# Another order of products in one stage of a TensorE-bound block, a root spread by two float32r products, and a bias moved to the output gate

## The chip, the cores and the metric

The kernel runs on one core of a Trainium2 chip. The metric is the device time of one execution, in microseconds (us). The profile of one execution gives, for each engine, when each instruction ran: TensorE (PE, with its weight loads PEld), VectorE (DVE), ScalarE (ACT), GpSimd (POOL) and the DMA-issuing SyncE (SP).

## What is computed

One block over 512 tokens of width 1024, in float32. The change lies in the middle part, the token mixer:

```python
h = RMSNorm(x); p = h @ w_in             # one input projection
r, k, v, w_lo, a_lo, g_lo = token_shift(p[:, :SHIFT_COLS], mu)   # u + (prev - u) * mu, columns of 512, 512, 512, 64-wide codes, ...
w_log = -softplus(-(w0 + tanh(w_lo) @ w_up)) - 0.5               # decay
a     = sigmoid(a0 + a_lo @ a_up)                                # rate
g     = sigmoid(g_lo) @ g_up
... delta-rule recurrence over 8 heads of 64, giving y ...
y = groupnorm(y) * lnx_g + lnx_b
y = (y + sum(r * k * r_k) * v) * g                               # bonus, output gate
```

A second mixer (forgetting attention), two SwiGLU layers and a final norm make up the rest.

## The kernel before

Everything is kept transposed: 128 features on the partitions, 512 tokens in the free dimension (P = 128, T = 512, KD = 8 slices of the model width, NB = 4 blocks of 128 tokens, NP = 4 pairs of heads). A float32 product is made of three float32r products: each operand is split into a rounded high part and the rest, and `mm3` (L174 to L176) adds hi*hi, lo*hi and hi*lo in one PSUM bank. The weights' split is `split_w`: ScalarE casts `raw` to `whi` (L166), VectorE subtracts to `wlo` (L167). `raw` has three buffers, filled by SP's queue; `whi` and `wlo` have two each. A projection column of 128 outputs is `mix.cols`: 8 slices of 3 products, 24 in all, into one bank named `pk` (mixer columns), `pl` (codes), `pgt` (gates) or `pq`.

The stage with the change begins near 340 us with the codes (`psa`, `psg`). VectorE and ScalarE make the mixer norm's reciprocal root for each token (`root`); TensorE spreads it over all partitions by a product with a matrix of ones (`spread_root`, tile `rows`), and VectorE copies it to `rstd`. Every later column is multiplied by `rstd` when it leaves its bank (tile `u`), then token-shifted by a ScalarE scale and a VectorE multiply-add (`shifted`). The codes go through tanh and a cast to the tile `codes`. Meanwhile TensorE makes the first pair's k column (weights at DA) and r column (at 0); their results go to `spare1`. Then four pairs of products with 96-row operands, the tiles `pz`, give decay and rate for the four pairs of heads (`uw`, `ux` are the up-projections, prepared by GpSimd; `za` holds the results), each followed by a sigmoid on ScalarE.

Four steps follow, `step(p)`, one for each pair of heads. Each has its columns k, r and v and one gate column `pgt`, the normalization of the keys (`ksq`, its parts `khi` and `klo`, the sum `pn`, and `krn`), the decayed products, the products `gp` of keys with queries (64 records of 64x64), and the bonus: `rk`, its parts `rhi` and `rlo`, the sum over a head by two products into `pn`, and `bon`, stored to `bsave` and read back at the end, where `shaped` and `opened` apply it and the gate. The third column of the first pair, v, takes the weights loaded in advance as `ready[2 * DA]`.

In this stage the order of each engine's instructions isn't written by hand: the tile framework's scheduler orders them from its own estimate of times, except where `tc.issue_after` (this instruction after that one on its engine) or `tc.keep_in_program_order` binds it. Every engine runs its instructions in that order. From about 500 us on the order is written out by hand.

Of the kernel before, what the change touches and what calls it, by code (L numbers as in the profile page):

```python
# [10 lines left out]
F32R = mybir.dt.float32r  # L11
BF16 = mybir.dt.bfloat16
AF = mybir.ActivationFunctionType
ALU = mybir.AluOpType
# [4 lines left out]
P = 128  # L19
T = 512  # L20
D = 1024
KD = D // P
DFF = 2816
KF = DFF // P
DA = 512
NP = DA // P
C = 32
NC = T // C
NB = T // P
# [4 lines left out]
PAR_FFN1, PAR_MIX, PAR_FFN2, PAR_MU = 0, 8, 16, 24  # L34
PAR_MUA, PAR_MUG = 36, 37
PAR_W0, PAR_A0, PAR_KK, PAR_KA, PAR_RK, PAR_LG, PAR_LB = 38, 42, 46, 50, 54, 58, 62
# [45 lines left out]
def kernel(  # L82
# [24 lines left out]
    dve, act, pe = [Queued(e, False) for e in (nc.vector, nc.scalar, nc.tensor)]  # L107
# [10 lines left out]
    pr = ctx.enter_context(tc.tile_pool(name="pr", bufs=3, space=PSUM))  # L118
    pf = ctx.enter_context(tc.tile_pool(name="pf", bufs=3, space=PSUM))
    dp = ctx.enter_context(tc.tile_pool(name="dp", bufs=1, space=DRAM))  # L120

    def bank(name, pool_=None):
        pool_ = pool_ or pm
        return pool_.tile([P, T], F32, tag="b", name=name)

    def tmp(name, shape=(P, T), dt=F32, tag="t", **kw):
        return tp.tile(list(shape), dt, tag=tag, name=name, **kw)


    ident = cp.tile([P, P], F32, name="ident")  # L130
# [3 lines left out]
    onesr = cp.tile([P, P], F32R, name="onesr")  # L134
    ones = onesr[:].bitcast(F32)
# [34 lines left out]
    def load_w(aps, kt, n, eng=None):  # L170
        return split_w(load_raw(aps, kt, n), kt, n, eng)
# [23 lines left out]
    def split(dst_hi, dst_lo, src, hi_eng="act"):  # L195
        cast = act.copy(dst_hi, src) if hi_eng == "act" else dve.tensor_copy(dst_hi, src)
        return cast, dve.tensor_tensor(dst_lo, src, dst_hi.bitcast(F32), op=ALU.subtract)

    def f32(ap):
        return ap.bitcast(F32)  # L200
# [7 lines left out]
    class Plan:  # L208
# [4 lines left out]
        def op(s, engine, us, do, *deps, rank=0, takes=(), frees=(), later=0.0, kind="w"):  # L213
            s.ops.append(dict(engine=engine, do=do, deps=deps, takes=takes, frees=frees, done=False))
            return s.ops[-1]
# [86 lines left out]
    def pc(i):  # L302
        return par[:, i:i + 1]
# [345 lines left out]
    class Wide:  # L649
# [231 lines left out]
        def root(s):  # L881
            nrm = s.nrm
            for i in range(2):
                pe.matmul(s.ssum[:], onesr[:], nrm.sum[i][:], start=i == 0, stop=i == 1)
            nrm.rstd = xp.tile([P, T], F32, tag="rstd", name="rstd")
            act.activation(nrm.rstd[:], s.ssum[:], AF.Ln, bias=epsr[:, 0:1], scale=1.0 / D)
            act.activation(nrm.rstd[:], nrm.rstd[:], AF.Exp, scale=-0.5)
            s.sa = [xp.tile([P, T], F32, tag="acc", name=f"sa{i}", bufs=2)[:] for i in range(2)]
# [83 lines left out]
    mix = Norm(PAR_MIX, 2)  # L972
# [45 lines left out]
    def root(rc):  # L1018
        dve.tensor_tensor(rc, sums[0][:], sums[1][:], op=ALU.add)
        act.activation(rc, rc, AF.Ln, bias=epsr[:, 0:1], scale=1.0 / D)  # L1020
        act.activation(rc, rc, AF.Exp, scale=-0.5)
        dg = tmp("dg")
        for b in range(NB):
            dve.tensor_scalar(dg[:, b * P:(b + 1) * P], ident[:], rc[:, b:b + 1], None, op0=ALU.mult)
        return dg

    def spread_root(dg, behind):
        ps = bank("rows", pr)
        with tc.issue_after(behind.ins):
            pe.matmul(ps[:], ones, dg[:], start=True, stop=True)  # L1030
        mix.rstd = xp.tile([P, T], F32, tag="rstd", name="rstd")
        dve.tensor_copy(mix.rstd[:], ps[:])

# [7 lines left out]
    op = o1.enter_context(tc.tile_pool(name="o1", bufs=1, side="right"))  # L1041
# [33 lines left out]
    def win(c0, n=P):  # L1075
        return [(0, W[:, c0:c0 + n])]

    nrm2 = Norm(PAR_FFN2)
    with ExitStack() as mx:
        rp = mx.enter_context(tc.tile_pool(name="rp", bufs=1))  # L1080
# [5 lines left out]
        def duo(tag, name, dt=F32):  # L1086
            return sp.tile([P, 2, T], dt, name=name, tag=tag)
# [3 lines left out]
        spare = [h[:, i] for h in (duo("RD2", "spare0"), duo("RD3", "spare1")) for i in range(2)]  # L1091
# [10 lines left out]
        def shifted(o, src, rows, mu):  # L1102
            act.activation(o[0:rows, :], src[0:rows, :], AF.Copy, scale=omu[0:rows, mu - PAR_MU:mu - PAR_MU + 1])
            dve.scalar_tensor_tensor(o[0:rows, 1:T], src[0:rows, 0:T - 1], pc(mu)[0:rows, :], o[0:rows, 1:T],
                                     op0=ALU.mult, op1=ALU.add)


        rc = rp.tile([P, NB], F32, name="rc")
# [28 lines left out]
        uw, ux = [lr.tile([96, DA], F32R, name=n) for n in ("uw", "ux")]  # L1137
# [13 lines left out]
        def normed(ps, rows=P):  # L1151
            u = tmp("u")
            dve.tensor_tensor(u[0:rows, :], ps[0:rows, :], mix.rstd[0:rows, :], op=ALU.mult)
            return u
# [13 lines left out]
        ready = {c0: load_w(win(c0), KD, P) for c0 in (DA, 0)}  # L1168
        act.on, act.last = True, None
        ready[2 * DA] = load_w(win(2 * DA), KD, P)  # L1170
        lw, lx = [codes[:, i] for i in range(2)]
# [6 lines left out]
        act.on = False  # L1178
        zslots = [h for g in G[3] for h in (g[:, 0:8], g[:, 8:16])] + [BKs[3][:, 0:8], BKs[3][:, 8:16]]
        zslots = [h.rearrange("p c a t -> p (c a t)") for h in zslots] + spare[0:2]  # L1180
        spread = []
        for o, c0, mu in ((spare[2], DA, 4), (spare[3], 0, 0)):
            ps = bank("pk", pf)
            spread = mix.cols(ps[:], *ready.pop(c0), P)
            shifted(o, normed(ps), P, PAR_MU + mu)
        za = []
        for p in range(NP):
            za.append((zslots[2 * p], zslots[2 * p + 1]))
            for i, (w_, x_, par0, o) in enumerate(((uw, lw, PAR_W0, zslots[2 * p]), (ux, lx, PAR_A0, zslots[2 * p + 1]))):
                ps = bank("pz", (pr, pf)[i])  # L1190
                with tc.issue_after(spread[2 * p + i].ins):
                    pe.matmul(ps[:], w_[0:96, p * P:(p + 1) * P], x_[0:96, :], start=True, stop=True)
                tc.keep_in_program_order(act.activation(o, ps[:], AF.Sigmoid, bias=pc(par0 + p)))
        logs = tc.keep_in_program_order(act.preload_act_table_set("natural_log_exp_and_others"))
        xctx.close()
        fctx = ExitStack()
        vtp = fctx.enter_context(tc.tile_pool(name="vtp", bufs=1, side="right"))
# [10 lines left out]
        vs = [V4[:, p] for p in range(NP)]  # L1208
# [10 lines left out]
        def work(name, dt=F32):  # L1219
            late = name in ("kka", "rk", "bon")  # L1220
            return t2.tile([P, T], dt, name=name, tag="sb" if late else "sa", bufs=3 if late else 5)
# [48 lines left out]
        def half(q):  # L1270
            return slice(q * 64, (q + 1) * 64)

        def step(p):
            if p % 3 == 0:
                k, r = spare[2], spare[3]
            else:
                k, r = [t2.tile([P, T], F32, name=f"{n}{p}")[:] for n in "kr"]
# [26 lines left out]
            ps = bank("pn", pf)  # L1304
# [20 lines left out]
            with tc.issue_after(mms[5].ins):  # L1325
                for c in range(NC):
                    for q in range(2):
                        o = half((q + c + 1) % 2)
                        gm = pe.matmul(gps[q][o, c // 2], BK[half(q), c], G[p][0][half(q), c], start=True, stop=True)
            for q in range(2):  # L1330
                for odd in range(2):
                    o = half((q + odd + 1) % 2)
# [4 lines left out]
                        op=ALU.mult)  # L1337
# [9 lines left out]
            ps = bank("pn", pr)  # L1347
# [4 lines left out]
                pe.matmul(ps[:], bonesr[:], lo[:], start=False, stop=True)  # L1352
            bon = work("bon")
            dve.tensor_tensor(bon[:], ps[:], v[:], op=ALU.mult)
            act.activation(bon[:], bon[:], AF.Identity, bias=pc(PAR_LB + p))
            nc.sync.dma_start(bsave[p], bon[:])

        for p in range(NP):
# [13 lines left out]
        for t in range(C - 1):  # L1372
            n, m = t + 1, C - 1 - t
# [82 lines left out]
        for b in range(NB):  # L1456
            o = vtp.tile([P, T], F32, name=f"vt{b}", tag=f"vt{b}")
# [39 lines left out]
        for q in range(2):  # L1497
            o = (1 - q) * 64
# [11 lines left out]
        for q in range(2):  # L1510
            o = (1 - q) * 64
# [9 lines left out]
        for q in range(2):  # L1521
            pool.memset(Rs[0][half(q), :, q, :], 0.0)
            for i in range(RN):
                o = (1 - q) * 64
# [6 lines left out]
        op = plan.op  # L1531
        summed, gone = [op("SP", 0.0, None, later=us, frees=frees) for us, frees in ((3.0, ()), (3.5, ["w"]))]
        o = op("ACT", 0.69, b1.log, summed, rank=SCAN, takes=["t"], frees=["pf"])
        o = op("ACT", 0.63, b1.root, o, rank=SCAN)
# [110 lines left out]
        for c in range(NC):  # L1645
# [4 lines left out]
            if c % 4 == 3 and c < NC // 2:  # L1650
                o = op("SP", 0.4, on(fetch, nc.sync, c + 5, 4), e, later=4.0)
# [15 lines left out]
        ready, weighed = {0: [summed], 1: [rooted]}, []  # L1667
# [72 lines left out]
        for m in range(NP + 3, 2 * KD):  # L1740
            g = Held()
            w, o = columns("pgt", COL_GA + m * P)
# [11 lines left out]
            o = op("DVE", 0.61, result, o, rank=NEXT, takes=["gs"], frees=["pm"])  # L1754
            if m + 1 < 2 * KD:
                o = op("ACT", 0.55 if tanhs else 1.84, opened, o, *roots, rank=ROWS)
# [150 lines left out]
        o = []  # L1907
        for p in range(NP):
            o = op("ACT", 0.63, on(part_y, p), *outs[p], *sees, *o, rank=FILL)
            o = [op("DVE", 0.69, on(part_l, p), o, rank=FILL)]  # L1910
# [29 lines left out]
        ycs, sqs, pgs, pus, parts = [None] * NP, [None] * NP, [None] * NP, [None] * NP, {}  # L1940
# [30 lines left out]
            dve.scalar_tensor_tensor(vs[p], vs[p], pc(PAR_LG + p), bons[p], op0=ALU.mult, op1=ALU.add)  # L1971

        def opened(p):
            dve.tensor_tensor(vs[p], vs[p], pus[p][:], op=ALU.mult)

        def halves_of(p):
            split(*ya[p], vs[p])
# [33 lines left out]
        ps = proj(0, fox_proj, ybs, fws[0])  # L2011
        for m in range(KD):
# [11 lines left out]
            if m + 1 < KD:  # L2024
                ps = proj(m + 1, fox_proj, ybs, fws[m + 1])
# [29 lines left out]
        for m in range(KD):  # L2055
            g = slot[m]
            ps = proj(m, rwkv_proj, ya)
# [4 lines left out]
        for m in range(KD):  # L2062
            wh, wl = load_w([(0, w_out[0][:, m * P:(m + 1) * P])], KD, P)
            ps = bank("pw")
# [68 lines left out]
    with tc.tile_pool(name="hp", bufs=1) as hp:  # L2133
# [14 lines left out]
        ps = [bank("pa"), bank("pb", pr)]  # L2148
# [54 lines left out]
```

## Time and profile before

| | us |
|---|---|
| median of 3 runs | 1086.06 (1086.01 to 1086.47) |
| the profiled execution: time | 1085.94 |
| the profiled execution: span from first to last instruction | 1083.9 |
| mean granted TensorE clock | 0.999 |
| the stage 340 to 500 us (codes, steps, inversion of the pair matrices): TensorE without work | 1.4 |

How to read the rows: in the order of time, a row has the start, the length, the engine, the line of the kernel, the operation, the tiles as out<-in, the shape and the count; in brackets stands how long the engine had been idle before it and what ended that. In the table by stage, each engine's busy time is followed by its count of instructions. Matmul records overlap: each is 0.39 us long, and steady ones start 0.23 us apart.

### The profile page before, as it was taken

The numbers are of one execution on the slowest core, as the hardware profiler recorded it, in microseconds if no ns is written. First come the engines' busy times: TensorE is split into PE (matmuls) and PEld (weight loads), VectorE is DVE, ScalarE is ACT, GpSimd is POOL, SyncE is SP. The second block draws the span as 40 slices with busy tenths as digits, with TensorE's granted clock in tenths as the row PEclk, the third lists the DMA queues.
The fourth block names the chain that finished last, engine by engine and source line by source line (L and its number), as shares of the span: only waits on it lengthen the run. The fifth ranks groups of instructions, "written<-read, shape, count | busy, mean of one in ns | idle before, by whom it ended". The sixth has DMA issues, their size and how long they took to land.

```text
span 1083.9 us, 16868 instructions
## 1 busy us (share of the span) xinstructions
PE 1074.8 (99%) x6378; PEld 883.9 (82%) x6378; DVE 833.2 (77%) x1155; ACT 673.7 (62%) x1055; POOL 212.5 (20%) x259
## 2 busy tenths in 40 slices
PE   9999999999999999999999999999999999999997
PEld 7888888888887887888788787888888888888886
DVE  7998576789865699888787777867597666699874
ACT  6765556576555766435889877524576555576554
POOL 1221220134203212402000130123311212114210
PEclk9999999999999999999999999999999999999999
DMA  7989988879945443444212354636967979869972
GB/s 219 255 171 235 209 170 201 189 146 188 232 127 168 114 112 106 124 136 114 82 46 82 99 154 128 195 116 202 245 156 176 205 202 185 191 151 203 236 188 78
DMA packets 142095, 177.13 MB, mean 163 GB/s; under 512 B 12094, under 2 KB 78206, under 8 KB 142014
## 3 DMA queue, kind: packets, MB, share of 16 engines
q0 software_dynamic: 33392, 70.14, 33.9%
q1 hardware_dynamic: 107886, 104.48, 31.5%
q10 hardware_dynamic: 736, 1.45, 0.3%
q8 instruction: 50, 0.82, 0.3%
q14 instruction: 31, 0.25, 0.1%
HBM read 163.51 MB, written 12.52 MB: 162 GB/s over the span
## 4 chain that ended last, share of the span: by engine, by line
PE 97%; DVE 1%; ACT 1%; issue 0%; DVEq 0%; ACTq 0%
PE P L102 40%; PE P L176 6%; PE P L174 6%; PE P L175 6%; PE pgt L102 5%; PE l L102 3%; PE spot L102 3%; PE pq L102 3%; PE ppj L102 2%; PE pk L176 2%; PE pk L174 2%; PE pk L175 2%; PE pb L102 2%; PE pa L102 2%; PE pw L175 1%; PE pw L174 1%
## 5 line engine op out<-in xcount | busy, mean ns | idle before, releaser
L102 PE MATMUL P<-sraw,q 128*128 128x512 f32 x344 | 91.3, 389 | 0.0
L102 PEld LDWEIGHTS P<-sraw,q 128*128 128x128 f32 x344 | 64.6, 188 | 13.4
L102 PE MATMUL P<-swhi,q 128*128 128x512 f32 x224 | 71.4, 390 | 0.0
L166 ACT CAST whi<-raw 128x1024 fp32r<-128x1024 f32 (+2 forms) x42 | 40.4, 962 | 48.8 <-issue 19.3
L102 PE MATMUL P<-sraw,wxh 128*128 128x512 f32 x200 | 68.4, 394 | 0.0
L102 PE MATMUL P<-swhi,wxh 128*128 128x512 f32 x144 | 56.9, 395 | 0.0
L102 PE MATMUL P<-swhi,wxl 128*128 128x512 f32 x144 | 56.1, 390 | 0.0
L102 PE MATMUL P<-swlo,wxh 128*128 128x512 f32 x144 | 56.1, 389 | 0.0
L167 DVE TENSOR_TENSOR wlo<-raw,whi 128x1024 fp32r<-128x1024 f32 (+2 forms) x43 | 48.4, 1127 | 9.6 <-ACT whi L166 8.5
L692 POOL DMA_DIRECT2D cb<-in_ffn_w_dram x20 | 24.1, 1203 | 150.8 <-DVE cd L102 85.1
L102 PE MATMUL P<-sraw,wxl 128*128 128x512 f32 x136 | 53.0, 390 | 0.0
L692 POOL DMA_DIRECT2D cd<-in_ffn_w_dram x24 | 29.5, 1230 | 102.5 <-DVE swlo L102 37.5
L102 PEld LDWEIGHTS P<-swhi,q 128*128 128x128 f32 x224 | 42.0, 188 | 8.7
L102 PE MATMUL P<-swlo,q 128*128 128x512 f32 x112 | 43.6, 389 | 0.0
L102 PEld LDWEIGHTS P<-sraw,wxh 128*128 128x128 f32 x200 | 37.2, 188 | 7.3
L102 ACT COPY RD<-spot 32x128 f32<-32x128 f32 (+2 forms) x128 | 39.9, 311 | 5.3 <-PE spot L102 2.3
L102 ACT CAST sraw<-cd 128x1024 fp32r<-128x1024 f32 x30 | 31.5, 1051 | 14.9 <-PE P L102 11.5
L102 DVE TENSOR_TENSOR swlo<-ca,swhi 128x1024 fp32r<-128x1024 f32 x24 | 29.2, 1221 | 14.0 <-ACT swhi L102 14.0
L102 DVE TENSOR_TENSOR u<-P,u 128x512 f32<-128x512 f32 x52 | 34.1, 683 | 5.8 <-ACT u L102 5.8
L176 PE MATMUL pk<-xh,wlo 128*128 128x512 f32 x96 | 37.5, 393 | 1.0 <-DVE wlo L167 1.0
L174 PE MATMUL pk<-xh,whi 128*128 128x512 f32 x96 | 38.0, 396 | 0.4 <-DVE u L1227 0.4
L102 DVE TENSOR_TENSOR swlo<-cc,swhi 128x1024 fp32r<-128x1024 f32 x20 | 24.5, 1224 | 18.0 <-ACT swhi L102 17.6
(623 smaller groups left out, 3418.9 us busy)
## 6 DMA issues: line engine op xcount, KB each, us to landing
raw<-in_w_in_dram SPq DMA_DIRECT2D x40, 512.0 KB
cc<-in_ffn_w_dram SPq DMA_DIRECT2D x36, 512.0 KB
cb<-in_ffn_w_dram POOLq DMA_DIRECT2D x36, 512.0 KB, 6.0
cb<-in_ffn_w_dram SPq DMA_DIRECT2D x32, 512.0 KB
cd<-in_ffn_w_dram POOLq DMA_DIRECT2D x32, 512.0 KB, 7.8
ca<-in_ffn_w_dram POOLq DMA_DIRECT2D x32, 512.0 KB, 7.4
ca<-in_ffn_w_dram SPq DMA_DIRECT2D x20, 512.0 KB
cd<-in_ffn_w_dram SPq DMA_DIRECT2D x18, 512.0 KB
```

Of the source, the lines that this page charges most:

```text
L102: q.last = do(*a, **kw)
L166: (hi_eng or act).copy(hi[:], raw[:])
L167: (eng or dve).tensor_tensor(lo[:], raw[:], hi[:].bitcast(F32), op=ALU.subtract)
L174: pe.matmul(ps, whi, xhi, start=first, stop=False, skip_group_check=onto)
L175: pe.matmul(ps, whi, xlo, start=False, stop=False, skip_group_check=onto)
L176: return pe.matmul(ps, wlo, xhi, start=False, stop=last, skip_group_check=onto)
L692: nc.gpsimd.dma_start(to, s.block(b, n, h), accum_op=ALU.add)
```

## The change

Three edits. In `root` the four diagonal blocks are no longer made one by one in float32: the root is split into a float32r pair, and two VectorE products with the identity make two float32r matrices, which `spread_root` adds by two products. The decay and rate products (`pz`) are issued one after each slice of the second column instead of after both columns, over three banks (two of the pool `pr`, one of `pf`), and the second column's shift comes behind the activation table's load in the program. The bonus loses its bias addition on ScalarE; the bias is now added in `opened`.

```diff
         act.activation(rc, rc, AF.Exp, scale=-0.5)
-        dg = tmp("dg")
-        for b in range(NB):
-            dve.tensor_scalar(dg[:, b * P:(b + 1) * P], ident[:], rc[:, b:b + 1], None, op0=ALU.mult)
-        return dg
+        rhl = rp.tile([P, 2, NB], F32R, name="rhl")
+        split(rhl[:, 0], rhl[:, 1], rc, "dve")
+        dgs = []
+        for i in range(2):
+            dgs.append(tmp("dg", dt=F32R))
+            dve.tensor_tensor(dgs[i][:].rearrange("p (b c) -> p b c", b=NB), ident[:].unsqueeze(1).broadcast_to([P, NB, P]),
+                              f32(rhl[:, i]).unsqueeze(2).broadcast_to([P, NB, P]), op=ALU.mult)
+        return dgs
...
         with tc.issue_after(behind.ins):
-            pe.matmul(ps[:], ones, dg[:], start=True, stop=True)
+            for i in range(2):
+                pe.matmul(ps[:], onesr[:], dg[i][:], start=i == 0, stop=i == 1)
...
-        spread = []
-        for o, c0, mu in ((spare[2], DA, 4), (spare[3], 0, 0)):
-            ps = bank("pk", pf)
-            spread = mix.cols(ps[:], *ready.pop(c0), P)
-            shifted(o, normed(ps), P, PAR_MU + mu)
-        za = []
-        for p in range(NP):
-            za.append((zslots[2 * p], zslots[2 * p + 1]))
-            for i, (w_, x_, par0, o) in enumerate(((uw, lw, PAR_W0, zslots[2 * p]), (ux, lx, PAR_A0, zslots[2 * p + 1]))):
-                ps = bank("pz", (pr, pf)[i])
-                with tc.issue_after(spread[2 * p + i].ins):
-                    pe.matmul(ps[:], w_[0:96, p * P:(p + 1) * P], x_[0:96, :], start=True, stop=True)
-                tc.keep_in_program_order(act.activation(o, ps[:], AF.Sigmoid, bias=pc(par0 + p)))
+        za = [(zslots[2 * p], zslots[2 * p + 1]) for p in range(NP)]
+
+        def rate(n, behind):
+            p, i = n // 2, n % 2
+            w_, x_, par0 = ((uw, lw, PAR_W0), (ux, lx, PAR_A0))[i]
+            ps = bank("pz", (pr, pf, pr)[n % 3])
+            with tc.issue_after(behind.ins):
+                m = pe.matmul(ps[:], w_[0:96, p * P:(p + 1) * P], x_[0:96, :], start=True, stop=True)
+            tc.keep_in_program_order(act.activation(za[p][i], ps[:], AF.Sigmoid, bias=pc(par0 + p)))
+            return m
+
+        ps = bank("pk", pf)
+        mix.cols(ps[:], *ready.pop(DA), P)
+        shifted(spare[2], normed(ps), P, PAR_MU + 4)
+        ps, ready_r, spread = bank("pk", pf), ready.pop(0), []
+        holes = []
+        for k in range(KD):
+            spread += mix.cols(ps[:], *ready_r, P, holes, [k], k == 0, k == KD - 1)
+            holes = [rate(k - 1, spread[-1])] if k else []
+        rate(KD - 1, holes[0])
         logs = tc.keep_in_program_order(act.preload_act_table_set("natural_log_exp_and_others"))
+        shifted(spare[3], normed(ps), P, PAR_MU)
...
             dve.tensor_tensor(bon[:], ps[:], v[:], op=ALU.mult)
-            act.activation(bon[:], bon[:], AF.Identity, bias=pc(PAR_LB + p))
...
-            dve.tensor_tensor(vs[p], vs[p], pus[p][:], op=ALU.mult)
+            dve.scalar_tensor_tensor(vs[p], vs[p], pc(PAR_LB + p), pus[p][:], op0=ALU.add, op1=ALU.mult)
```

Since the scheduler orders this stage, instructions move that the diff does not touch. Three places follow. Tile numbers differ between the two kernels; a pk number stands for one column.

TensorE before, where the second column (pk_2741) ends and the third column, v (pk_2842, weights whi_2702 and wlo_2703), begins:

```order
L174 MATMUL pk_2741<-xh6_2478,whi_2696 128x512
L175 MATMUL pk_2741<-xl6_2479,whi_2696 128x512
L176 MATMUL pk_2741<-xh6_2478,wlo_2697 128x512
L174 MATMUL pk_2842<-xh0_2584,whi_2702 128x512
L175 MATMUL pk_2842<-xl0_2585,whi_2702 128x512
L176 MATMUL pk_2842<-xh0_2584,wlo_2703 128x512
```

TensorE after the change, where the third column (pk_2845, weights whi_2705 and wlo_2706) begins; the second column is pk_2744:

```order
L174 MATMUL pk_2744<-xh0_2584,whi_2699 128x512
L175 MATMUL pk_2744<-xl0_2585,whi_2699 128x512
L176 MATMUL pk_2744<-xh0_2584,wlo_2700 128x512
L174 MATMUL pk_2744<-xh0_2584,whi_2699 128x512
L175 MATMUL pk_2744<-xl0_2585,whi_2699 128x512
L176 MATMUL pk_2744<-xh0_2584,wlo_2700 128x512
L174 MATMUL pk_2845<-xh0_2584,whi_2705 128x512
L175 MATMUL pk_2845<-xl0_2585,whi_2705 128x512
L176 MATMUL pk_2845<-xh0_2584,wlo_2706 128x512
```

The third column has moved ahead of slices 3 to 8 of the second: it now begins 30 products after the root's spread instead of 48. All its 24 products follow each other, and after them the second column goes on with a pz product before each slice of three, and the first gate column (pgt) begins before the last of them.

ScalarE before, around tanh (L1164) and sigmoid (L1165) of the codes and the cast of the third column's weights:

```order
L1103 ACTIVATE la_2670<-u_2676,omu_2559 64x512
L1103 ACTIVATE lg_2671<-u_2680,omu_2559 96x512
L1164 ACTIVATE la_2670<-la_2670 32x512
L1165 ACTIVATE lg_2671<-lg_2671 96x512
L102 CAST whi_2702<-raw_2700 128x1024
L102 CAST codes_2550<-la_2670 32x512 x4
```

ScalarE after the change, at the same place:

```order
L1108 ACTIVATE la_2673<-u_2679,omu_2559 64x512
L1108 ACTIVATE lg_2674<-u_2683,omu_2559 96x512
L1169 ACTIVATE la_2673<-la_2673 32x512
L102 CAST whi_2705<-raw_2703 128x1024
L1170 ACTIVATE lg_2674<-lg_2674 96x512
L102 CAST codes_2550<-la_2673 32x512 x4
```

The cast has passed the sigmoid, and still stands behind tanh.

TensorE before, around the third step's pair products gp; the pk column there is the fourth step's second:

```order
L176 MATMUL pk<-xh_2444,wlo 128x512
L174 MATMUL pk<-xh_2444,whi 128x512
L1329 MATMUL gp<-G_2542,BK_2548 64x64 x32
L1351 MATMUL pn<-rhi,bonesr 128x512
L1352 MATMUL pn<-rlo,bonesr 128x512
L175 MATMUL pk<-xl_2445,whi 128x512
```

TensorE after the change, around the same gp; the pk column is the fourth step's first:

```order
L176 MATMUL pgt<-xh_2478,wlo 128x512
L174 MATMUL pk<-xh_2584,whi 128x512
L175 MATMUL pk<-xl_2585,whi 128x512
L1342 MATMUL gp<-G_2542,BK_2548 64x64 x32
L1364 MATMUL pn<-rhi,bonesr 128x512
L1365 MATMUL pn<-rlo,bonesr 128x512
L176 MATMUL pk<-xh_2584,wlo 128x512
```

The gp block and the two bonus products behind it (32 program lines, 64 records) have moved ahead of 38 products: they now stand two products into the fourth step's first column, ahead of its first product with wlo, instead of 16 products into the second.

## The prediction, on record before the run

> **What bounds the kernel now.** I read the page first (busy time, then the chain that ended last), then busy time by stage, then each engine's order of time between 344 and 475 us, where nearly all of the change lies.
>
> ```profile
> PE 1074.8 (99%) x6378; PEld 883.9 (82%) x6378; DVE 833.2 (77%) x1155; ACT 673.7 (62%) x1055; POOL 212.5 (20%) x259
> PE 97%; DVE 1%; ACT 1%; issue 0%; DVEq 0%; ACTq 0%
> ```
>
> TensorE is busy for 1074.8 of 1083.9 us and carries 97% of the chain. So only two things move the time: a change in TensorE's own work, or in the moments at which it stands. By stage:
>
> ```profile
> 380.00:460.00 80.00, 78.99 (x578) 63.76 (x577) 70.74 (x97) 46.99 (x65) 19.47 (x35) 1.00 0.41 116
> 500.00:640.00 140.00, 140.00 (x1825) 112.73 (x1823) 106.98 (x263) 115.42 (x293) 10.47 (x19) 1.00 0.29 80
> 640.00:760.00 120.00, 120.00 (x623) 98.01 (x623) 91.44 (x127) 64.44 (x103) 24.29 (x28) 1.00 0.53 168
> ```
>
> The columns after the window's length are the busy times of PE, PEld, DVE, ACT and POOL. From 500 to 760 us TensorE shows no idle time at all, so a delay made before 500 us goes through to the end one for one. Between 380 and 460 us VectorE is 88% busy, close behind. TensorE stands three times in the stretch that the change reorders:
>
> ```profile
> 374.05 0.40 PE L176 MATMUL pgt<-xh,wlo 128*128 128x512 f32 x1
> 374.82 0.50 PE L174 MATMUL pk<-xh,whi 128*128 128x512 f32 x1 [0.37 <-DVE u L1227]
> 375.15 0.40 PE L175 MATMUL pk<-xl,whi 128*128 128x512 f32 x1
> ...
> 423.92 0.40 PE L175 MATMUL pk<-xl,whi 128*128 128x512 f32 x1
> 424.65 0.50 PE L176 MATMUL pk<-xh,wlo 128*128 128x512 f32 x1 [0.34 <-DVE wlo L167]
> 424.99 0.40 PE L174 MATMUL pk<-xh,whi 128*128 128x512 f32 x1
> ...
> 430.00 0.39 PE L175 MATMUL pk<-xl,whi 128*128 128x512 f32 x1
> 431.06 0.50 PE L176 MATMUL pk<-xh,wlo 128*128 128x512 f32 x1 [0.68 <-DVE wlo L167]
> 431.40 0.39 PE L174 MATMUL pk<-xh,whi 128*128 128x512 f32 x1
> ```
>
> The idle times in brackets understate the loss, because the product after a wait also starts late. From starts, with 0.23 us for a steady product: 375.15 - 374.05 - 0.46 = 0.64, 424.99 - 423.92 - 0.46 = 0.61, 431.40 - 430.00 - 0.46 = 0.94, together 2.19 us. That, and what the root's product can save, is all that can be won.
>
> **The root's spread.** One full-precision product becomes two float32r products.
>
> ```profile
> 349.72 1.02 PE L1030 MATMUL rows<-dg,onesr 128*128 128x512 f32 x2
> 350.18 0.79 PE L174 MATMUL pk<-xh,whi 128*128 128x512 f32 x1
> 350.81 0.39 PE L175 MATMUL pk<-xl,whi 128*128 128x512 f32 x1
> 351.04 0.40 PE L174 MATMUL pk<-xh,whi 128*128 128x512 f32 x1
> ...
> 357.43 0.39 PE L174 MATMUL pk<-xh,whi 128*128 128x512 f32 x1
> ...
> L1024 DVE TENSOR_SCALAR dg<-ident,rc x4: 278/284/315, 346.7 to 347.3; 128x128 f32<-128x128 f32 x4
> ```
>
> From 349.72 to 351.04 pass the root's product and two pk products: 1.32 - 0.46 = 0.86 us for the root. Two float32r products take 0.46, so TensorE gains 0.40. On VectorE four dg products (0.87 us) become a cast and a subtraction of 128x4 and two 128x512 products, some 0.3 + 1.3 us by its 0.6 us for a product of that size (below). They end near 348.3, and TensorE takes them up at 349.72 behind the pl products: hidden, 1.4 us to spare.
>
> **The third column, moved ahead of the second column's end.** The rows of the order shown with the change say that TensorE now does the second column's first six products, then the whole third column, and only then the eight pz products between the rest of the second column. ScalarE's cast of the third column's weights (whi) stands between tanh (L1164) and the sigmoid. What they wait for:
>
> ```profile
> 355.25 1.35 POOL L1146 TENSOR_TENSOR ux<-loraw,ux 32x512 fp32r<-32x512 f32 x1
> 355.48 1.66 DVE L1104 SCALAR_TENSOR_TENSOR la<-u,par,la 64x511 f32<-64x511 f32 x1
> 357.07 0.73 DVE L1104 SCALAR_TENSOR_TENSOR lg<-u,par,lg 96x511 f32<-96x511 f32 x1
> 357.18 0.63 ACT L1164 ACTIVATE la<-la 32x512 f32<-32x512 f32 x1 [1.75 <-DVE la L1104]
> 357.73 0.67 DVE L1153 TENSOR_TENSOR u<-pk,rstd 128x512 f32<-128x512 f32 x1
> 357.84 0.64 ACT L1165 ACTIVATE lg<-lg 96x512 f32<-96x512 f32 x1
> 358.38 1.03 ACT L102 CAST whi<-raw 128x1024 fp32r<-128x1024 f32 x1
> 359.45 1.23 DVE L167 TENSOR_TENSOR wlo<-raw,whi 128x1024 fp32r<-128x1024 f32 x1 [1.04 <-ACT whi L102]
> ```
>
> Before, TensorE reaches this column after 48 products, past 361 us, and all is ready. Now it arrives after 30. Thirty products took from 350.58 (the first pk's steady place, 350.81 - 0.23) to 357.43, so 6.85 us; from 350.18 they end at 357.03. The cast cannot start before tanh is through: 357.18 plus the 0.54 at which ScalarE's instructions follow each other (357.84 to 358.38) is 357.72, and it ends at 358.76. TensorE stands from 357.03 to about 358.9 (0.05 to 0.15 for the restart, as in the waits above): 1.85 us. Two products later it needs wlo, which VectorE starts at 358.80 and ends at 360.03; TensorE would be there at 359.35: another 0.8. **The new wait costs 2.7 us.** Bounds: la's shift took 1.66 us where lg's took 0.73 while GpSimd worked on ux; without that meeting tanh comes 0.93 earlier and the wait is 1.75; with one more GpSimd operation of that sort ahead of it, 1.0 later, it is 3.7. I take 2.7, because la ended 0.54 after ux did and a shift of la's start by up to 1.1 us leaves its end there.
>
> Queued behind the cast are the sigmoid of lg, its store on SP's queue and the codes; the first pz product stands 22 products after wlo, near 365.2, and the codes are cast by about 362: covered. The last pz product comes 33 products later, at 372.7, and the next column 17 after that, at 376.6.
>
> ```profile
> 374.07 0.69 DVE L1227 TENSOR_TENSOR u<-pk,rstd 128x512 f32<-128x512 f32 x1 [4.85 <-PE pz L1192]
> ```
>
> This u frees the third column's bank and waited for the last pz. Here the last pz is through by 373.1, u then ends near 375, and TensorE asks for the bank at 376.6: the wait of 0.64 goes.
>
> **Later in the four steps.** The scheduler's other moves put the third step's pair products gp, and the bonus sum pn behind them, 38 products earlier, ahead of the first wlo of the fourth step's first column. That wlo was the wait of 424.65; it is now ready before rlo, which VectorE makes last, so the wait becomes one for rlo; the wlo of 431.06 follows rlo by some 2 us, with 22 products (5 us) before it is needed: gone. For rlo:
>
> ```profile
> 421.67 1.22 DVE L1293 TENSOR_TENSOR_SCAN spare<-cmask,spare 128x512 f32<-128x512 f32 x1
> ...
> 437.43 2.83 DVE L1333 TENSOR_TENSOR G<-gp,gmask 64x512 f32<-64x512 f32 x4
> 440.30 0.69 DVE L1354 TENSOR_TENSOR bon<-pn,V 128x512 f32<-128x512 f32 x1
> ...
> 442.11 1.22 DVE L167 TENSOR_TENSOR wlo<-raw,whi 128x1024 fp32r<-128x1024 f32 x1
> 443.24 0.68 DVE L1301 TENSOR_TENSOR BK<-spare,Pi 128x512 f32<-128x512 f32 x1
> 443.84 0.74 DVE L1104 SCALAR_TENSOR_TENSOR spare<-u,par,spare 128x511 f32<-128x511 f32 x1
> ...
> 434.16 0.39 PE L174 MATMUL pk<-xh,whi 128*128 128x512 f32 x1
> ...
> 435.91 0.39 PE L1352 MATMUL pn<-rlo,bonesr 128*128 128x512 f32 x1
> ```
>
> From the third step's klo to its rlo VectorE has the masks (2.87 from start to start), two wlo and a scan (1.13 each), 13 others at 0.60 and rlo itself (0.69): 14.8 us without a pause. TensorE needs between the same two 51 products (11.6) and the gp block (435.91 - 434.16 - 0.46 = 1.29): 12.9. If both leave klo together TensorE waits 2.0; if klo is ready 2 us ahead, nothing. No row places them; I take the middle, 1.0.
>
> **The bonus.** Four ScalarE additions go, and the output gate's products take a third operand.
>
> ```profile
> L1355 ACT ACTIVATE bon<-bon,par x4: 710/724/726, 406.0 to 457.3; 128x512 f32<-128x512 f32 x4
> L102 DVE TENSOR_TENSOR V<-V,pg x4: 676/682/689, 660.9 to 679.3; 128x512 f32<-128x512 f32 x4
> ```
>
> The four (2.9 us) lie on an engine 59% busy, and their stores on SP's queue now wait for VectorE, 0.7 us sooner than for ScalarE; the weight loads queued behind these stores wait for a wlo that ends later still. Nothing of it lies on the path. The four products may go from 0.68 to about 0.74 each; TensorE had no idle time there: nothing.
>
> **The sum**: -0.40 - 2.19 + 2.7 + 1.0 = +1.1 us. On the profiled execution (1085.94) that gives 1087.0; the median of the runs is 0.12 above it, so 1087.2.
>
> [...]
>
> **Rivals.**
> *Slower by over 0.2%.* The wait at the third column is longer, since tanh is later. Place: la's shift behind a GpSimd operation. VectorE now has wlo and low between dg and rstd, and each meeting with GpSimd costs about 0.9 (1.66 against 0.73). Price one for one. It decides when tanh starts after 358.25, 1.07 past its old place; two meetings more (1.9) give +3.0, 1089.1. Against it: rstd needs no more than the old 350.85.
> *The rlo wait does not come.* +0.1, 1086.2. For it: TensorE is already late by 2.7 and VectorE gets time to catch up. Against it: that run has no pause to shorten.
> *The third column finds its weights.* Tanh would have to start by 355.4; then -0.40 - 2.19 + 1.0 = -1.6, 1084.5, and with no rlo wait -2.6, 1083.5. Against it: la's row.
>
> **How the numbers follow.** 0.2% is 2.2 us, about what a measurement can tell from no change. Forecast 0.48, slower rival 0.23, no rlo wait 0.23, weights in time 0.06. The slower side holds the second. Faster by 0.2% needs the last with all in its favour: 0.03. The rest is the same: 0.74. The range goes from a wait of 1.75 with no rlo wait (-0.40 - 2.19 + 1.75 = -0.8, 1085.2) to 3.7 with the rlo wait at 2.0 (+3.1, 1089.2).
>
> **What the profile after would show.** Right: the rows product in two records 0.23 apart; TensorE idle near 357 for ScalarE's whi and at about 359.4 for VectorE's wlo, 2.7 in all; no wait for u near 376; one for rlo near 428; the 500 to 760 us stages shifted whole. Wrong: no idle near 357, tanh ahead of 356 or after 358.3, or TensorE idle past 500.

## The result, and the profile after

The changed kernel takes 1090.75 us in the median (1090.52 to 1091.43), the kernel before 1086.06: 0.43% slower, ratio 1.0043 with a 95% interval of 1.003 to 1.0057. The forecast was 1087.2, range 1085.2 to 1089.2, so 3.6 us too low. The profiled execution took 1091.43 us with a span of 1089.7. Three single executions of 1192 to 3380 us, one of the kernel before and one each of two kernels below, are no part of the ratios given here.

From the page of the kernel after, busy time and the chain that ended last:

```profile
PE 1077.4 (99%) x6378; PEld 884.1 (81%) x6378; DVE 833.6 (76%) x1155; ACT 671.7 (62%) x1051; POOL 212.9 (20%) x259
PE 96%; DVE 2%; ACT 1%; issue 0%; DMA 0%; DVEq 0%; ACTq 0%
```

TensorE is busy 2.6 us longer and VectorE carries one point more of the chain: some new time is waiting, and some is the products themselves. To see where, I took each product's start in the two traces, in order, and subtracted. 0.74 us of the difference is there at 340 us, before anything was changed (this execution is 0.7 above the median of its kernel), and is left out:

| start before, us | 356 | 362 | 380 | 440 | 475 | 503 | 680 | 747 and later |
|---|---|---|---|---|---|---|---|---|
| later after the change, us | -0.25 | 2.30 | 1.75 | 1.28 | 1.63 | 3.34 | 3.27 | 5.05 |
| by the forecast's terms | -0.40 | 2.30 | 1.66 | 1.11 | 1.11 | 1.11 | 1.11 | 1.11 |

Up to 440 us the forecast holds to 0.2 us. Two steps behind it, at 503 us and from 680 to 747 us, were not in it, and neither was a small one of 0.35 ahead of 475 us. The stage that was forecast, from the order of time of the kernel after (start, length, engine, line, operation, tiles; idle time in brackets):

```profile
357.69 0.39 PE L176 MATMUL pk<-xh,wlo 128*128 128x512 f32 x1
359.51 0.50 PE L174 MATMUL pk<-xh,whi 128*128 128x512 f32 x1 [1.44 <-ACT whi L102]
359.85 0.40 PE L175 MATMUL pk<-xl,whi 128*128 128x512 f32 x1
360.77 0.50 PE L176 MATMUL pk<-xh,wlo 128*128 128x512 f32 x1 [0.53 <-DVE wlo L167]
...
357.90 0.63 ACT L1169 ACTIVATE la<-la 32x512 f32<-32x512 f32 x1 [1.75 <-DVE la L1109]
358.43 1.03 ACT L102 CAST whi<-raw 128x1024 fp32r<-128x1024 f32 x1
...
426.94 1.16 PE L1342 MATMUL gp<-G,BK 64*64 64x64 f32 x64 [0.30 <-DVE BK L1329]
429.25 0.50 PE L1365 MATMUL pn<-rlo,bonesr 128*128 128x512 f32 x1 [0.72 <-DVE rlo L197]
```

TensorE stands for whi and then for wlo of the third column, in all 2.55 us from 356 to 362 us. The waits for u (374.82) and wlo (424.65, 431.06) are gone; rlo is waited for, and BK just ahead of it.

The first step that was missed. First the kernel before, then the kernel after, from the last store of the pair matrices (Ld) to the product that takes the first l:

```profile
456.88 0.65 POOL L1341 DMA_DIRECT2D Ld<-G  x1 [0.75 <-DVE G L1333]
459.52 0.57 POOL L1365 DMA_DIRECT2D Ls<-Ld  x1
460.23 0.96 POOL L1368 MEMSET TT<- 128x1024 f32 x1
463.61 0.19 DVE L1375 TENSOR_TENSOR prod<-TT,Ls 128x31 f32<-128x31 f32 x1 [3.35 <-DMA Ls<-Ld]
499.63 0.69 DVE L102 TENSOR_TENSOR l<-qsq,h 128x512 fp32r<-128x512 f32 x1
501.73 0.39 PE L102 MATMUL pq<-l,bonesr 128*128 128x512 f32 x1
```

```profile
460.62 0.65 POOL L1354 DMA_DIRECT2D Ld<-G  x1 [0.75 <-DVE G L1346]
464.50 0.97 POOL L1380 MEMSET TT<- 128x1024 f32 x1 [2.49 <-DMA bsave<-bon]
466.81 0.57 POOL L1377 DMA_DIRECT2D Ls<-Ld  x1
472.32 0.19 DVE L1387 TENSOR_TENSOR prod<-TT,Ls 128x31 f32<-128x31 f32 x1 [5.70 <-DMA Ls<-Ld]
504.95 0.69 DVE L102 TENSOR_TENSOR l<-qsq,h 128x512 fp32r<-128x512 f32 x1
505.70 0.50 PE L102 MATMUL pq<-l,bonesr 128*128 128x512 f32 x1 [1.43 <-DVE l L102]
```

Before, l was ready at 500.32, 1.4 us ahead of its product. After, GpSimd's memset of TT has come ahead of the load of Ls in its queue and waits for the last store of the bonus (bsave); the inversion on VectorE begins 8.7 us later, l 5.3 later. TensorE itself comes only some 2.4 us later (these three with the 0.74 in them): it waits. The small step of 0.35 belongs here too: a gate column's wlo, which VectorE makes between the first products of the late inversion (474.35 to 475.57), is taken late at 475.63, and in the run below with GpSimd's queue mended this step is gone.

The second: the same 45 products apart in both kernels, before and then after:

```profile
690.00 0.39 PE L176 MATMUL ppj<-ya,wlo 128*128 128x512 f32 x1
...
700.21 0.39 PE L176 MATMUL ppj<-ya,wlo 128*128 128x512 f32 x1
```

```profile
690.07 0.39 PE L176 MATMUL ppj<-ya,wlo 128*128 128x512 f32 x1
...
700.57 0.40 PE L176 MATMUL ppj<-ya,wlo 128*128 128x512 f32 x1
```

10.21 / 45 = 0.2269 us a product before, 10.50 / 45 = 0.2333 after, with no idle time and the granted clock at 1.00 in both. This holds for the products of the two output projections (ppj, pw) that take ya, mh or ml: 1.8 us, from 3.27 to 5.05 in the table.

### The profile page after: what moved, and what is told of

Same layout as the page of the kernel before. It is cut to its first block, busy times and chain, and to the rows that moved or that the text cites. A ratio compares the mean times of both kernels' runs of the same rounds, so it can differ in the third digit from the quotient of the medians.

```text
span 1089.7 us, 16866 instructions
## 1 busy us (share of the span) xinstructions
PE 1077.4 (99%) x6378; PEld 884.1 (81%) x6378; DVE 833.6 (76%) x1155; ACT 671.7 (62%) x1051; POOL 212.9 (20%) x259
## 4 chain that ended last, share of the span: by engine, by line
PE 96%; DVE 2%; ACT 1%; issue 0%; DMA 0%; DVEq 0%; ACTq 0%
PE P L102 39%; PE P L174 5%; PE P L175 5%; PE P L176 5%; PE pgt L102 5%; PE l L102 3%; PE spot L102 3%; PE pq L102 3%; PE ppj L102 2%; PE pk L176 2%; PE pk L175 2%; PE pk L174 2%; PE pb L102 2%; PE pa L102 2%; PE pw L174 1%; PE pw L176 1%
```

## The experiments

Each was timed beside the kernel before (medians 1085.85 to 1086.15).

**One edit at a time, and the tile alone.** The tile rhl (32 bytes on each partition) lies in the pool rp, and every tile allocated behind it there and in the stage's own pool moves by 32 bytes. Four kernels from the one before: the tile alone; the root's edit; the rates' edit; the bonus edit.

```diff
+        rp.tile([P, 2, NB], F32R, name="rhl")      # the first kernel: never used
         dg = tmp("dg")
```

> The kernel before, with an unused tile of 32 bytes per partition in the pool rp where the change makes rhl; the order of every engine's instructions is that of the kernel before. Theory (addresses): the tile moves every later tile of the pool and all tiles of the stage's own pools by 32 bytes, and the products of the two output projections (680 to 747 us) then start 0.2333 us apart instead of 0.2267, some 270 of them: +1.75 us, 1087.8. Rival (the slower pitch comes from the new order or from the new operand of the output gate's products): pitch 0.2267, 1086.1.

Measured 1087.74 us, ratio 1.0015 (1.0006 to 1.0024); 0.2333 us from product to product (the pitch) from 690 to 740 us. The theory holds: an unused tile costs 1.65 us.

> The kernel before with only the root's spread changed. Theory (addresses, and 0.40 won on the root): -0.40 + 1.75 = +1.35, with +-0.6 for waits that its small changes of order make, 1087.4; pitch 0.2333 from 680 to 747 us. Rival (the root's edit only saves): -0.4, 1085.7, pitch 0.2267. Both: no wait for l near 504 us.

Measured 1087.66, ratio 1.0015 (1.0006 to 1.0024), pitch 0.2333: the theory. The root's gain was 0.2 in the trace at 356 us, and the wait for u was 0.24 longer.

> The kernel before with only the decay and rate products moved. Theory (three separate prices): the stage from 350 to 480 us loses what the changed kernel lost there without the root's gain, 1.6 + 0.4 = +2.0, with waits for whi and wlo near 357 to 360 us and for rlo near 428 us; no wait for l near 504 us, pitch 0.2267: 1088.1. Rival (the late inversion, and the wait for l behind it, come from this edit because the fourth step ends later): the wait for l of about 1.7 is here too, 1089.8. The forecast on record would be +1.5 for this edit, 1087.6.

Measured 1089.74, ratio 1.0032 (1.002 to 1.0045): the rival's time, but not its cause. The wait for l was 0.18 and the pitch 0.2267, so neither of the other costs is in it. TensorE lost 4.6 us by 362 us and won 0.8 back later. By busy time from 361 to 364 us, the rates' edit alone, then the changed kernel (columns as in the table by stage, the granted clock behind POOL's column):

```profile
361.00:364.00 3.00, 3.00 (x8) 2.32 (x8) 1.87 (x3) 2.13 (x4) 0.00 (x0) 0.50 0.64 175
```

```profile
361.00:364.00 3.00, 3.00 (x14) 2.45 (x14) 1.87 (x3) 2.11 (x5) 0.00 (x0) 1.00 0.87 224
```

After a stand of 2.0 us for whi (1.6 in the changed kernel), the clock was granted at half from 360.88 to 364.29 us, and the products started 0.43 us apart. Of the 2.0 us by which this stretch is longer than in the changed kernel, the stand makes 0.4 and the clock 1.6.

> The kernel before with only the bonus bias moved to the output gate. Theory (GpSimd's queue): the load of Ls now stands behind the memset of TT, which waits for the last store of the bonus; the inversion begins 7 to 8 us later than before, TensorE waits about 1.7 us for l near 504 us: 1087.8. Rival (the forecast on record: the bonus edit lies beside the path): 1086.1, no wait for l.

Measured 1086.23, ratio 1.0002 (0.9993 to 1.0011). The rival holds for this edit alone: the queue is turned round as in the changed kernel, but l starts at 501.32 us, still in time.

**The tile's size, the memset, the third column, the clock.**

```diff
-        rhl = rp.tile([P, 2, NB], F32R, name="rhl")
+        rhl = rp.tile([P, 4, NB], F32R, name="rhl")
```

> The changed kernel with rhl made 64 bytes per partition instead of 32, so that every tile behind it lies 64 bytes further than in the kernel before, not 32; the order of every engine is that of the changed kernel. Theory (the place of a tile counts by its remainder of 64 bytes): pitch 0.2267 from 690 to 740 us, 1090.75 - 1.7 = 1089.0. Rival (any move from the old places costs, by another period or by a collision of tiles): pitch 0.2333, 1090.7.

Measured 1089.97, pitch 0.2292: neither. Not every move costs alike, and the period isn't 64 bytes.

```diff
+        with tc.issue_after(ls.ins):               # ls: the load of Ls
-        pool.memset(TT[:], 0.0)
+            pool.memset(TT[:], 0.0)
```

> The changed kernel with GpSimd's memset of TT bound behind the load of Ls; TensorE's order is the same. Theory (GpSimd's queue and the late fourth step together): Ls is issued about 3 us sooner, the inversion begins near 469 us instead of 472.3, less than 6 us later than in the kernel before, and the wait for l at 504 to 506 us (1.7 us) goes but for 0.2: 1089.1. Rival (l is late for another reason, since with the bonus edit alone there was no such wait): the wait stays, 1090.7.

Measured 1089.99. The wait for l fell by half, to 0.75 in starts: klc's memset, next in the queue, took over the wait for bsave.

Both of these, and the third column behind the second:

```diff
-            mms = mix.cols(ps[:], *(...), P)
+            mms = mix.cols(ps[:], *(...), P, [spread[-1]] if (c0, p) == (2 * DA, 0) else [])
```

> The changed kernel with rhl of 64 bytes, the memset of TT behind the load of Ls, and the third column's first product bound behind the second column's last. Theory (three prices that add up): 1090.75 - 1.7 - 1.7 leaves 1087.4 for the first two; the third column's wait of 2.5 goes as well: 1084.9, with +-1 for the waits of the new order behind it. Rival (the scheduler puts an equal wait elsewhere in the four steps): 1087.4.

Measured 1090.38, worse than the rival; of that, 1.2 us are the price of this edit, since the other two had brought only 0.8 each. With the third column held back, the first product of the rates came due instead, whose codes were not ready, and half clock followed:

```profile
361.09 0.47 PE L1193 MATMUL pz<-codes,uw 96*128 96x512 f32 x1 [3.56 <-ACT codes L102]
```

So the scheduler had only filled a hole: behind 30 products neither the rates' codes nor the third column's weights are there.

The rates' edit alone, with the sigmoid of lg and its store moved behind the cast of the third column's weights (the store's line is left out here):

```diff
-        act.activation(lg[0:96, :], lg[0:96, :], AF.Sigmoid)
...
         ready[2 * DA] = load_w(win(2 * DA), KD, P)
+        act.activation(lg[0:96, :], lg[0:96, :], AF.Sigmoid)
```

> The kernel before with the decay and rate products moved, and ScalarE's cast of the third column's weights ahead of the sigmoid of lg (as it stands in the changed kernel); nothing else differs from the run with the rate edit alone, in which TensorE stood 2.0 us for the cast and then ran at half clock (0.50 granted) from 361 to 364 us. Theory (a stand of about 2 us at this place halves the clock, one of 1.5 us doesn't): the stand is 0.54 shorter and the clock stays at 1.00: 1089.7 - 0.5 - 1.8 = 1087.4. Rival (the clock's fall doesn't hang on the length of the stand): half clock again, 1089.2.

Measured 1088.67, ratio 1.0022 (1.0013 to 1.0031), with single runs from 1087.24 to 1089.86. The stand was 1.3 us, and the profiled execution (1088.96) ran at half clock all the same, from 360.94 to 364.35 us; the fastest was 1.7 us quicker. A stand of 1.3 us did not guard against it.

**The memsets of TT and klc both behind the load of Ls.**

```diff
         for q in range(2):
-            pool.memset(f32(klc[q][:]), 0.0)
+            with tc.issue_after(ls.ins):
+                pool.memset(f32(klc[q][:]), 0.0)
```

> The changed kernel with the memset of TT and the two of klc bound behind the load of Ls on GpSimd (in the run before, with TT alone, klc's first memset took over the wait for the store of the bonus, and Ls came only 1.0 us sooner). Theory (GpSimd's queue and the late fourth step together): Ls is issued near 463 us, the inversion begins near 467 us, the wait for l at 504 us goes: 1090.75 - 1.7 = 1089.1. Rival (most of that wait is not the queue's): it stays at 0.8 as with TT alone, 1090.0.

Measured 1089.43, ratio 1.0031 (1.0019 to 1.0042). The inversion begins 4.2 us sooner than in the changed kernel, and of the wait for l 0.17 is left, by starts from 500 to 503 us:

```profile
463.38 0.57 POOL L1377 DMA_DIRECT2D Ls<-Ld  x1
468.07 0.19 DVE L1388 TENSOR_TENSOR prod<-TT,Ls 128x31 f32<-128x31 f32 x1 [2.32 <-DMA Ls<-Ld]
502.23 0.69 DVE L102 TENSOR_TENSOR l<-qsq,h 128x512 fp32r<-128x512 f32 x1
```

**The rates over the third column.** With rhl of 128 bytes, and the queue mended:

```diff
-        ps, ready_r, spread = bank("pk", pf), ready.pop(0), []
-        holes = []
+        ps = bank("pk", pf)
+        spread = mix.cols(ps[:], *ready.pop(0), P)
+        psv, ready_v, third, holes = bank("pk"), ready.pop(2 * DA), [], [spread[-1]]
         for k in range(KD):
-            spread += mix.cols(ps[:], *ready_r, P, holes, [k], k == 0, k == KD - 1)
-            holes = [rate(k - 1, spread[-1])] if k else []
+            third += mix.cols(psv[:], *ready_v, P, holes, [k], k == 0, k == KD - 1)
+            holes = [rate(k - 1, third[-1])] if k else []
```

> The changed kernel with the decay and rate products between the slices of the third column instead of the second, rhl of 128 bytes, and the memsets of TT and klc behind the load of Ls. Theory (TensorE loses where it comes to weights or codes before ScalarE has made them, about 359 to 362 us; a tile's place counts by its remainder of 128 bytes): no wait near 357 us, clock 1.00 from 361 to 364 us, pitch 0.2267 from 690 to 740 us, no wait for l: 1086.1 - 0.2 for the root and between -2.2 and +1.5 for the old and new waits of the four steps, 1085.5. Rival (the waits come back in another place of the stage): 1087.4 or more.

Measured 1088.02: the rival. No stand near 357 us and the clock at 1.00, but waits of 0.64 (whi of the first gate column, 363.24) and 1.16 (gs, 376.57) in their place; and the pitch is 0.2327: 128 bytes are no period either.

**Weights and operands moved together; 96 bytes.** Here 32 bytes stand ahead of all pools but the first:

```diff
     onec = cp.tile([P, 1], F32, name="onec")
+    cp.tile([P, 8], F32, name="lead8")
```

> The kernel before with 32 unused bytes ahead of all pools, so that weights and moving operands move together by 32 bytes in the whole program; all orders as before. Theory R (the pitch hangs on where the moving operand lies against the weights, modulo 128 bytes): pitch 0.2267 as before, 1086.1. Theory A (it hangs on the moving operand's own remainder): some 4000 full-width products start 0.2333 apart, +27 us, 1113.

Measured 1086.81, ratio 1.0006 (0.9997 to 1.0015). Theory R: ya has moved by 32 bytes as in the first kernel, and its products start 0.2268 apart, since the weights have moved too. The few operands that did not move, yh and yl in pools allocated from the other end, became slow against the moved weights: 10 products there, 2.33 us. From 655 to 690 us this makes the 0.6 by which this kernel is slower.

```profile
675.68 0.40 PE L102 MATMUL ppj<-yl,whi 128*128 128x512 f32 x1
...
678.01 0.40 PE L102 MATMUL ppj<-yh,wlo 128*128 128x512 f32 x1
```

```diff
+        rp.tile([P, 6, NB], F32R, name="rhl")      # never used
```

> The kernel before with an unused tile of 96 bytes where rhl stands; all orders as before. With +32 bytes the pitch of the output projections was 0.2333, with +64 (changed kernel, rhl of 64 bytes) 0.2292. Theory (only the distance from the old place modulo 128 bytes counts, alike on both sides): 0.2333, 1087.8. Rival (it grows or falls steadily with the remainder): 0.2267 to 0.2292, 1086.1 to 1086.7.

Measured 1087.96, pitch 0.2333 in the mean as the theory says, but 0.2312 to 0.2368 by operand.

**No tile moved; then no stand; then the kernel before without its own wait.** The first keeps rhl in the tile la, which is written only later:

```diff
-        rhl = rp.tile([P, 2, NB], F32R, name="rhl")
+        rhl = la[:, 0:2 * NB].bitcast(F32R).rearrange("p (i b) -> p i b", i=2)
```

> The changed kernel with rhl kept in the first 32 bytes of the tile la, so that no tile moves, and the memsets of TT and klc behind the load of Ls; the order of TensorE, ScalarE, GpSimd and SP is that of the run with the memsets alone (1089.4). Theory (place of the tiles, GpSimd's queue and the stage from 350 to 440 us add up): pitch 0.2267 from 690 to 740 us, 1089.4 - 1.7 = 1087.7. Rival (the slow pitch hangs on something else of the changed kernel besides): 0.229 or more, 1088.3 to 1089.4.

Measured 1087.87, ratio 1.0017 (1.0009 to 1.0026), pitch 0.2267: the theory.

With the rates over the third column as above, and:

```diff
-            u = t2.tile([P, T], F32, name="u", tag="u", bufs=3)
+            u = tmp("u") if (c0, p) == (2 * DA, 0) else t2.tile([P, T], F32, name="u", tag="u", bufs=3)
...
-            gate.go()
+            gate.go(behind=third[-1] if m == 0 else ())
```

> As the run before it, and the decay and rate products between the slices of the third column instead of the second, the first gate column behind the third, and the third column's tile u in a buffer that does not wait for the up-projections. Theory (what is left of the cost is the third column's stand of 2.5 us and the rlo wait of 1.5): no stand near 357 us; the waits for BK and rlo near 427 to 430 us stay, as gp stands at the same place: 1087.7 - 2.5 = 1085.2. Rival (TensorE stands as long elsewhere before 380 us): 1087 or more.

Measured 1085.24, ratio 0.999 (0.9981 to 0.9999). TensorE does not stand before 420 us; the waits for BK (0.31) and rlo (0.72) stay. The theory, within 0.1 us.

The last is the kernel before with the root's edit, the line for rhl and the line for u:

> The kernel before with the root's spread changed (rhl inside la), and the third column's tile u in a buffer that does not wait for the up-projections; rates, bonus and GpSimd's queue as before. By the order the third gp block stands two products into the fourth step's second column. Theory (TensorE's own waits are all there is to win): 0.2 on the root, 0.64 at 374.82 us, 1.5 at 424 to 431 us, pitch 0.2267: 1086.1 - 2.4 = 1083.7. Rival (the rlo or wlo waits stay in the new order): 1085.3.

Measured 1084.61, ratio 0.9984 (0.9975 to 0.9993): the fastest of all, 1.5 us below the kernel before and 6.1 below the changed one. It lies between the theory and the rival, because two waits stayed:

```profile
424.09 0.50 PE L176 MATMUL pk<-xh,wlo 128*128 128x512 f32 x1 [0.33 <-DVE wlo L167]
430.18 1.16 PE L1334 MATMUL gp<-G,BK 64*64 64x64 f32 x64 [0.34 <-DVE BK L1321]
```

## Why the prediction was wrong

Undone one after the other, there are three costs: the queue 1090.75 - 1089.43 = 1.3, the tile's place 1089.43 - 1087.87 = 1.6 (1.65 when added alone), and 1087.87 - 1086.09 = 1.8 for the stage that the prediction was about, where it said 1.1. Such differences add up to the whole by construction; the traces give each size a second time. By starts the queue costs 2.06 from 440 to 503 us, of which 0.2 stays when it is mended, and the tile's place 1.78. In the trace of the run that keeps the third cost alone, with the clock at full throughout, TensorE loses 1.47 between 345 and 747 us, 0.19 of it still at l. The 1.8 of its median agrees with that: three of its eleven executions had a mean granted clock of 0.997 (last section) and took 1088.71 to 1089.86 us, and without them the median is 1087.62, 1.5 above the kernel before.

**The root** gained 0.25 by 356 us, not 0.40. Two records 0.23 apart came as said; but the first wlo was now late by some 0.15.

**The third column** was right, in the mechanism too: 2.55 lost against 2.7, for ScalarE's cast behind tanh and then for wlo. The run without the stand was 2.6 faster. Tanh started at 357.90, which without the 0.74 is 357.16, as before (357.18). La's shift took 1.66 us in both, beside GpSimd's last operation on ux, which started at 355.96, 355.22 without the offset, against 355.25 before. What the shift takes without that operation is not shown, so the 0.93 of the prediction's bounds stays the author's estimate. The two dg products were through at 349.02 us, just ahead of GpSimd's first operation on uw:

```profile
347.73 1.29 DVE L1027 TENSOR_TENSOR dg<-ident,rhl 128x512 fp32r<-128x512 f32 x2
349.04 0.60 POOL L1145 CAST uw<-loraw 32x512 fp32r<-32x512 f32 x1
```

**The later waits** were right in sum: all three old ones went, and from 380 to 440 us the shift fell by 0.47 where -1.55 + 1.0 = -0.55 was said. The rlo wait stands where it was foretold; a part is already taken by BK ahead of gp. That its size fits is luck: the 1.0 was the middle between 0 and 2.0, and no row placed it.

**The rivals.** The time came out on the slower side, but not by that rival: tanh wasn't late. The other two did not occur.

**The step that failed** is the one that ends the sum before 500 us. From "TensorE shows no idle time at all" between 500 and 760 us the prediction took that nothing new arises there: "500 to 760 us stages shifted whole". That a delay made earlier goes through one for one is true, since the 3.34 of 503 us are still there, as 3.27, at 680. But 1.7 us were added at 503 us and 1.8 from 680 to 747 us. What the prediction named as a sign against itself, "TensorE idle past 500", is the row at 505.70. The step took "no idle time" for "nothing can become late". Two things were under it:

- Of the bonus edit the prediction said "Nothing of it lies on the path", having gone through ScalarE, VectorE and SP's queue; GpSimd's queue was not gone through. There the memset of TT passed the load of Ls. The cover was the 1.4 us that l had in hand. Alone the bonus edit uses 1.1 of them (l at 501.32, less 0.55 of offset, against 499.63) and costs nothing. The root's edit alone uses nearly as much: l ends at 501.89 and is taken at 502.13, so 0.24 is left. The rates' edit alone uses all of it and costs 0.18 there. All three together lose 2.1 by the starts from 440 to 503 us; with the queue mended, 0.2 of it is left. The queue's turn thus makes 1.9 by starts (1.3 by the medians), which no single edit shows. The bonus and the rates' edit without the root's were not run.
- A new tile was costed by its instructions alone, not by where it moves the tiles behind it. Nothing in the trace of before could price that; but the list of the tiles that move was to be had from the code.

## What to carry to other kernels

Where a stage shows no idle time, look for each operand from another engine how long it had been ready before it was taken: that margin, here 1.4 us, is the cover, and edits that are free one by one can use it up together. Go through every queue that a scheduler reorders, GpSimd's too, for an instruction that has come to stand behind one that waits for a DMA: here the load of Ls, 1.3 us by the medians. And in an allocation where products run at their shortest distance, 0.2267 us here, even a new tile of 32 bytes (1.65 us alone) belongs into room that is there already, or behind everything else.

## What the hardware showed that was not expected

**The distance in time of full-width float32r products changed with where the moving operand lies against the weights.** In the kernel before, the operands of the projections (xh, xl, yh, yl, ya, mh, ml) all lie a multiple of 256 bytes from whi, by the addresses in the compiled program (whi at 71712, ya at 139808; in the changed kernel 71712 and 139840). For ya against whi and wlo the distance in time was 0.2267 us unmoved, 0.2333 at +32 bytes, 0.2292 at +64, 0.2318 and 0.2368 at +96, 0.2334 at +128, and 0.2268 with both moved by 32; for yh and yl it was 0.2332 where the weights alone had moved by 32. The 0.2292 at +64 and the 0.2334 at +128 exclude a period of 64 or 128 bytes. No larger move was run, and the mechanism stays open.

**Stands of 1.3 to 2 us halved the clock for 3.41 us in some traces and not in others, by how they fell on steps of that length.** The kernel with no tile moved and the stand left in ran from 1087.15 to 1089.86 us in eleven runs, with mean granted clocks of 0.999 to 0.997; without the stand from 1084.61 to 1085.77. In the traces the granted clock changes a whole number of steps of 3.413 us after it first went to full: in the kernel before it is full from 6.40 to 1081.60 us, 315 steps; in the changed kernel from 7.54 to 1086.16 us, 316 steps; with the rates' edit alone from 5.89 us, with half clock from 104 to 105 steps later, 360.88 to 364.29. That start differs between these executions, so a stand near 357 to 361 us can fall into one step (2.39 us of it with the rates' edit alone) or be shared by two (1.04 and 0.93 in the changed kernel):

| kernel | TensorE idle in the step that has most of the stand, us | granted clock in the next step |
|---|---|---|
| third column held back | 2.88 | 0.50 |
| rates' edit alone | 2.39 | 0.50 |
| rates' edit alone, sigmoid moved | 1.71 | 0.50 |
| changed kernel with the memset of TT moved; with rhl of 64 bytes | 1.37; 1.36 | 1.00 |
| changed kernel with no tile moved; with the memsets of TT and klc moved | 1.27; 1.26 | 1.00 |
| changed kernel | 1.04 (and 0.93 in the next) | 1.00 |

In the changed kernel the two parts make 1.97 us and cost no clock; 1.71 us in one step did. In these eight traces 1.37 us idle or less in a step of 3.41 us left the clock at 1.00, and 1.71 us or more was followed by 0.50; nothing between was run.
